# Two of the gMLP's four ways down computed with Strassen's seven products

## The chip, the cores and the metric

One Trainium2 chip, of which the kernel uses a single core. A core has five engines that each work through an instruction list of their own, in order: TensorE (matmuls, with its weight loads beside them), VectorE, ScalarE, GpSimd and SyncE, which here issues the loads from memory. They meet through semaphores. In the profile they are PE, PEld, DVE, ACT, POOL and SP. The metric is the device time of one execution in microseconds, lower is better.

## What is computed

A trunk of two layers over 512 tokens of width 1024, in fp32. Layer 0 mixes with an mLSTM, layer 1 with a chunked gMLP, and each layer has a SwiGLU FFN before and after its mixer, a gated input embedding, and a LayerNorm after every residual. The change lies in the gMLP:

```python
def gmlp_mixer(x, w_in, b_in, vn_g, vn_b, ws, bs, w_out):      # x: 1 x 512 x 1024
    u, v = jnp.split(jax.nn.gelu(x @ w_in + b_in, approximate=False), 2, axis=-1)   # 2048 each
    v = layer_norm(v, vn_g, vn_b).reshape(B, NB, GM_BLOCK, GM_GROUPS, GM_GDIM)
    s = jnp.einsum('gts,bnsgc->bntgc', ws_m, v) + bs.T[:, :, None]   # within blocks of 128 tokens
    return (u * s.reshape(B, S, GM_WIDTH)) @ w_out               # 2048 -> 1024: the way down
...
x = layer_norm(DN_ALPHA * x + mix, ln_g[i, 1], ln_b[i, 1])
```

## The kernel before

**Precision.** Every fp32 matrix is held as a high and a low half in fp32r. `split` makes them: ScalarE copies the high half, VectorE subtracts it from the source. A product of two blocks is three matmuls (`mm3`): high by high, high by low, low by high. A matmul takes a 128 x 128 block as stationary operand and 512 columns as moving one.

**Weights.** The class `Weights` streams all weights through one list, `W.order`. A load of 1 MB goes from SyncE into one of three raw buffers (`wraw`), and is cut into tiles of 1024 columns. `fill` splits the next tile of the list as soon as a split buffer is free: four of kind main and two of kind extra in this stage. `release` gives a buffer back and fills at once; with `later=True` it is only noted, and `refill` fills later. With `low="dma"` the low half is not made by VectorE: ScalarE writes the source negated and rounded, and a DMA that GpSimd issues adds the source to it. A raw buffer is free for the next load when the last tile in it is split.

**The gMLP.** First `v` for all tokens, tokens on the partitions, four column chunks by four token blocks, into `gvf`. Then 16 gate blocks of 128 channels. For block b, `spatial(b)` multiplies the split `v` by the spatial weights into two banks (`sps`), VectorE adds bias and gain in four evictions (`gs`) after one small instruction (`gadd`), and `split_v(b + 2)` splits `v` for two blocks on. `gate_u(b + 1)` then makes the next block's gate columns: 24 matmuls into one bank (`gups`), a Gelu by ScalarE (`guf`). Last `gated(b)` multiplies the two and splits the result into `hh` and `hl`. After every fourth block `down` multiplies the four blocks by their four row blocks of `w_out`: for each of four token blocks, four row blocks by two halves of 512 columns by three matmuls into two banks (`dps`), and two residual additions by VectorE into `xt`. The last way down carries the LayerNorm along.

**Banks.** PSUM has eight banks of 512 columns. Four are handed out by `up_bank` (`ps_up`, one pool of four), four by `dn_bank` (`ps_dn`), which can pin them. `spatial` takes up banks, for blocks 1, 3 and 15 down banks.

**Strassen in the other stages.** The FFNs, and the mLSTM for its first three heads, take their ways down group by group through the class `Group`. The two factors are cut two by two; seven products of half-size sums replace eight. `form` makes the next activation sum (none, one or two additions by VectorE, in place) and splits it; `W.forms` makes the seven weight sums, two of them pairs of subtractions in place in the raw buffers; `product` runs one product into two pinned banks, and `add` adds them to `xt`. One product follows each up-projection, so that these steps are spread.

Of the kernel before, what the change touches and what calls it, by code (L numbers as in the profile page):

```python
# [237 lines left out]
def hybrid_trunk(ctx: ExitStack, tc, x, p, ln_g, ln_b, ffn1_wgu, ffn1_wd, ffn2_wgu, ffn2_wd,  # L238
# [20 lines left out]
    ps_up = ctx.enter_context(tc.tile_pool(name="ps_up", bufs=4, space=PSUM))  # L259
# [15 lines left out]

    def up_bank(name):
        return ps_up.tile([P, 512], F32, name=name, tag="up")
# [31 lines left out]
    def kp(w):  # L309
        return w.rearrange("(kb p) c -> p kb c", p=P)  # L310
# [58 lines left out]

    def stage_kinds(first):  # L370

        n = len(W.order) - first
        for i in range(n):
            extra = i % 6 >= 4 if i < n // 6 * 6 else i >= n - 2
            W.order[first + i] = ("extra" if extra else "main",) + W.order[first + i][1:]

    def ml_weights():
        win, wout = ml_w_in[0], ml_w_out[0]
        first = len(W.order)
        for h in range(HEADS):  # L380
# [7 lines left out]
            if h:  # L388
# [3 lines left out]
                j0, j1 = W.add_load(kp(wout)[:, k:k + 2, :], 3), W.add_load(kp(wout)[:, k + 2:k + 4, :], 3, "gb")  # L392
                left, right = ((slice(None), slice(None), slice(c, c + 512)) for c in (0, 512))
                down_w = W.forms("", (j0, left), (j0, right), (j1, right), (j1, left))
# [9 lines left out]
    def gm_weights():  # L404
        win, wout = gm_w_in[0], gm_w_out[0]
        first = len(W.order)
        for c in range(4):
            add_wide(win, GW + c * 512)
        for b in range(16):
# [4 lines left out]
            if b and b % 4 == 0:  # L414
                add_rows(wout, b - 4, 4)
# [314 lines left out]
    class Group:  # L730
# [5 lines left out]
        def __init__(self, h, pool, first=False):  # L736
            self.h, self.pool, self.half = h, pool, h.shape[1] // 2
# [26 lines left out]
        def product(self):  # L764
# [437 lines left out]
    def gmlp():  # L1202
        with stage_pool("extra", EXTRA) as extra, stage_pool("gm_parts") as near, stage_pool("ghpool", 4) as hpool, \
                stage_pool("gm") as mp:
            W.open("extra", extra, EXTRA)
            vf = mp.tile([P, TB, GW], F32, name="gvf")
# [34 lines left out]
            for c in range(4):  # L1241
# [9 lines left out]
                for t in range(TB):  # L1251
# [4 lines left out]
                    dst = vf[:, t, c * 512:(c + 1) * 512]  # L1256
# [7 lines left out]
                    if c == 3:  # L1264
# [5 lines left out]
                        vec.tensor_scalar(vf[:, t], vf[:, t], mv[:, 0:1], rs[:, 1:2], op0=OP.subtract, op1=OP.mult)  # L1270
# [12 lines left out]
            def split_v(b):  # L1283
# [5 lines left out]
                split(vh, vl, vf[:, :, b * P:(b + 1) * P])  # L1289
# [24 lines left out]
            def gated(s, uf):  # L1314
                vec.tensor_mul(s, s, uf)
# [178 lines left out]
```

## Time and profile before

| | us |
|---|---|
| time, median of 3 runs | 2232.23 |
| lowest and highest of them | 2232.04 to 2232.97 |
| the profiled execution's own time | 2232.51 |
| its span in the profile | 2230.8 |
| TensorE busy (PE) | 2220.3 |
| VectorE busy (DVE) | 1526.0 |
| ScalarE busy (ACT) | 913.9 |

The profile is of one execution. Times in it count from the start of its span. An engine's busy time is the union of its instructions' times; matmuls overlap in the pipeline, so their recorded lengths (389 ns) are longer than the distance from one start to the next. Views show the instructions in order of time, the waits with what ended them, busy times by stretch, and the DMAs with the time to their landing.

### The profile page before, as it was taken

What the parts mean: (1) busy time and instruction counts of PE and PEld (TensorE: products, weight loads), DVE (VectorE), ACT (ScalarE), POOL (GpSimd) and SP (SyncE); (2) the same over time, 40 slices, a digit from 0 to 9 for tenths busy, and PEclk for the clock granted to TensorE, in tenths of its full rate; (3) what the DMA queues carried; (4) which work ended last, traced back from release to release, by engine and by line L of the source; (5) the groups of instructions that cost most, each with busy time, mean ns of one, the idle gap of its engine ahead of it and who ended that gap; (6) DMA issues with size and microseconds to landing.
All of it is one profiled execution on the core that took longest, in us unless ns stands there. A gap on an engine that the chain in (4) does not pass through costs nothing.

```text
span 2230.8 us, 26548 instructions
## 1 busy us (share of the span) xinstructions
PE 2220.3 (100%) x10589; PEld 1864.0 (84%) x10589; DVE 1526.0 (68%) x2240; ACT 913.9 (41%) x1298; POOL 101.8 (5%) x135
## 2 busy tenths in 40 slices
PE   9999999999999999999999999999999999999998
PEld 8888888888888888888889888888888888888887
DVE  5666667777776786666687666666666578666677
ACT  4333336454646533333255333334343453333332
POOL 1000000111101100000000000000010100000000
PEclk9999999999999999999999999999999999999999
DMA  7422323466847443332233422223355443332221
GB/s 231 130 93 88 95 85 100 100 149 135 166 107 161 123 139 126 95 104 67 95 123 122 133 86 87 93 87 109 106 142 142 104 151 123 122 113 85 85 85 57
DMA packets 202723, 253.56 MB, mean 114 GB/s; under 512 B 5812, under 2 KB 156468, under 8 KB 202600
## 3 DMA queue, kind: packets, MB, share of 16 engines
q1 hardware_dynamic: 168080, 211.83, 29.5%
q0 software_dynamic: 27904, 25.35, 7.9%
q10 hardware_dynamic: 6616, 14.69, 2.0%
q8 instruction: 83, 1.36, 0.2%
q14 instruction: 40, 0.33, 0.0%
HBM read 224.58 MB, written 2.11 MB: 102 GB/s over the span
## 4 chain that ended last, share of the span: by engine, by line
PE 99%; ACT 1%; DVE 0%; issue 0%; DVEq 0%; POOL 0%; POOLq 0%
PE fps L269 13%; PE fps L270 13%; PE fps L268 13%; PE gps L270 7%; PE gps L269 7%; PE gps L268 7%; PE dps L269 3%; PE dps L268 3%; PE dps L270 3%; PE gups L268 1%; PE vps L268 1%; PE zps L268 1%; PE zps L270 1%; PE vps L270 1%; PE gvps L268 1%; PE gups L269 1%
## 5 line engine op out<-in xcount | busy, mean ns | idle before, releaser
L268 PE MATMUL fps<-xh,whi 128*128 128x512 f32 x1312 | 510.7, 389 | 0.0
L269 PE MATMUL fps<-xl,whi 128*128 128x512 f32 x1312 | 510.5, 389 | 0.0
L270 PE MATMUL fps<-xh,wlo 128*128 128x512 f32 x1312 | 510.4, 389 | 0.0
L199 DVE TENSOR_TENSOR wlo<-wraw,whi 128x1024 fp32r<-128x1024 f32 (+1 forms) x286 | 345.4, 1218 | 149.5 <-ACT whi L193 147.8
L193 ACT ACTIVATE whi<-wraw 128x1024 fp32r<-128x1024 f32 (+1 forms) x334 | 346.5, 1048 | 185.8 <-PE fps L269 81.6
L199 DVE TENSOR_TENSOR wlo<-wquarter,whi 128x1024 fp32r<-128x1024 f32 (+1 forms) x140 | 156.5, 1118 | 218.2 <-ACT whi L193 218.2
L268 PEld LDWEIGHTS fps<-xh,whi 128*128 128x128 f32 x1312 | 246.3, 188 | 51.2
L269 PEld LDWEIGHTS fps<-xl,whi 128*128 128x128 f32 x1312 | 246.3, 188 | 51.1
L270 PEld LDWEIGHTS fps<-xh,wlo 128*128 128x128 f32 x1312 | 246.2, 188 | 51.0
L193 ACT ACTIVATE whi<-wquarter 128x1024 fp32r<-128x1024 f32 (+1 forms) x140 | 136.3, 974 | 279.8 <-PE gps L270 209.0
L270 PE MATMUL gps<-whi,flo 128*128 128x512 f32 x588 | 229.3, 390 | 0.0
L268 PE MATMUL gps<-whi,fhi 128*128 128x512 f32 x588 | 229.3, 390 | 0.0
L269 PE MATMUL gps<-wlo,fhi 128*128 128x512 f32 x588 | 229.2, 390 | 0.0
L593 DVE TENSOR_TENSOR xt<-xt,gps 128x512 f32<-128x512 f32 x282 | 180.3, 680 | 0.5 <-PE gps L270 0.5
L817 ACT ACTIVATE sg<-fps 128x512 f32<-128x512 f32 x80 | 47.9, 598 | 228.4 <-PE fps L270 228.4
L273 ACT ACTIVATE fhi<-h 128x512 fp32r<-128x512 f32 (+1 forms) x140 | 80.5, 581 | 142.9 <-DVE h L755 54.4
L269 PEld LDWEIGHTS gps<-wlo,fhi 128*128 128x128 f32 x588 | 110.4, 188 | 23.5
L268 PEld LDWEIGHTS gps<-whi,fhi 128*128 128x128 f32 x588 | 110.4, 188 | 23.3
L270 PEld LDWEIGHTS gps<-whi,flo 128*128 128x128 f32 x588 | 110.4, 188 | 23.3
L274 DVE TENSOR_TENSOR flo<-h,fhi 128x512 fp32r<-128x512 f32 (+1 forms) x140 | 87.2, 634 | 42.9 <-ACT fhi L273 42.9
L563 POOL TENSOR_TENSOR rs<-rs,eps_pow 128x1 f32<-128x1 f32 x32 | 20.6, 643 | 1556.4 <-DVE rs L562 1556.4
L466 ACT ACTIVATE xf<-xps,cols 128x128 f32<-128x128 f32 x160 | 59.8, 453 | 52.5 <-PE xps L461 52.5
(289 smaller groups left out, 3736.4 us busy)
## 6 DMA issues: line engine op xcount, KB each, us to landing
wraw<-in_ffn_wgu_dram SPq DMA_DIRECT2D x79, 1024.0 KB, 6.0
wquarter<-in_ffn_wd_dram SPq DMA_DIRECT2D x64, 512.0 KB, 3.7
wraw<-in_ml_w_in_dram SPq DMA_DIRECT2D x24, 1024.0 KB, 5.5
wlo<-wraw POOLq DMA_DIRECT2D x48, 512.0 KB, 6.5
wraw<-in_gm_w_in_dram SPq DMA_DIRECT2D x15, 1024.0 KB, 5.7
wraw<-in_ffn_wgu_dram SPq DMA_DIRECT2D x17, 512.0 KB, 4.0
wraw<-in_ffn_wd_dram SPq DMA_DIRECT2D x8, 1024.0 KB, 4.9
wraw<-in_ml_w_out_dram SPq DMA_DIRECT2D x8, 1024.0 KB, 4.9
```

The costliest lines, as they stand in the source:

```text
L193: self.nc.scalar.activation(hi[:, s], src[:, s], AF.Copy)
L199: self.nc.vector.tensor_sub(lo[:, s], src[:, s], hi[:, s].bitcast(F32))
L268: mm(ps, st[0], mv[0], start=start, stop=False, skip_group_check=more)
L269: mm(ps, st[0], mv[1], start=False, stop=False, skip_group_check=more)
L270: mm(ps, st[1], mv[0], start=False, stop=stop, skip_group_check=more)
L273: sca.activation(hi, src, AF.Copy)
L274: vec.tensor_sub(lo, src, hi.bitcast(F32))
L466: sca.activation(xf[:, k], ps[:, k], AF.Identity, scale=col("ln_g", norm.at + 4 * g + k), bias=col("ln_b", norm.at + 4 * g + k))
L563: pool.tensor_tensor(rs[:, 1:2], rs[:, 0:1], eps_pow, op=OP.pow)
L593: vec.tensor_add(dst, dst, ps)
L817: sca.activation(sg, ps, AF.Silu)
```

## The change

- The first eight gate blocks, two groups of four, go down by `Group`'s seven products each. `GM_STEPS` says how many products follow the gate columns of each block: one after blocks 3, 4, 6 and 8 to 12, two after blocks 5, 7 and 13. The activations are cut by tokens (`by_tokens`), the row blocks of `w_out` into left and right halves of two loads, both into raw buffers.
- `gated` writes its product in place of `v` in `gvf`, which is cut into three tiles, so that blocks 10 to 13 can reuse the first two for `h`. From block 8 on `split_gated` splits; `h` has two pairs of buffers of its own where it had four, and blocks 14 and 15 use the forms' buffers.
- In blocks 1 to 12 the weight buffers are noted as free (`later=True`) and filled a block later, after the next block's spatial part.
- The third way down (blocks 8 to 11) comes after block 13, where it came after block 11.
- `up_bank` names its four banks and hands them out in turn; `stage_kinds` marks main and extra by another formula.

```diff
-    ps_up = ctx.enter_context(tc.tile_pool(name="ps_up", bufs=4, space=PSUM))
+    ps_up = ctx.enter_context(tc.tile_pool(name="ps_up", bufs=1, space=PSUM))
...
+    up_order = deque(range(4))
+
     def up_bank(name):
-        return ps_up.tile([P, 512], F32, name=name, tag="up")
+        up_order.rotate(-1)
+        return ps_up.tile([P, 512], F32, name=name, tag=f"up{up_order[-1]}")
...
+    GM_STEPS = {3: 1, 4: 1, 5: 2, 6: 1, 7: 2, 8: 1, 9: 1, 10: 1, 11: 1, 12: 1, 13: 2}
+    GM_LAST = max(GM_STEPS)
...
-            extra = i % 6 >= 4 if i < n // 6 * 6 else i >= n - 2
+            extra = i % 6 >= 4 if i < n - 4 else i >= n - 2
...
+    def two_row_forms(w, kind="raw"):
+        j0, j1 = W.add_load(w[:, :2], 3), W.add_load(w[:, 2:], 3, kind)
+        left, right = ((slice(None), slice(None), slice(c, c + 512)) for c in (0, 512))
+        return W.forms("", (j0, left), (j0, right), (j1, right), (j1, left))
...
-            if b and b % 4 == 0:
-                add_rows(wout, b - 4, 4)
+        tiles = W.order[at:]
+        del W.order[at:]
+        down_w, k = deque(), 0
+        for b, tile_b in enumerate(tiles):
+            W.order.append(tile_b)
+            for _ in range(GM_STEPS.get(b - 1, 0)):
+                if not down_w:
+                    down_w.extend(two_row_forms(kp(wout)[:, k:k + 4, :]))
+                    k += 4
+                W.order.append(down_w.popleft())
+            if b == GM_LAST + 1:
+                add_rows(wout, 8, 4)
...
+                if self.by_tokens:
+                    return self.h[:, 2 * i - 2:2 * i, (j - 1) * 256:j * 256]
...
-                    mm3(ps, [a[:, k, e * P:(e + 1) * P] for a in f], [a[:, k] for a in w],
+                    i, j = (e, k) if self.by_tokens else (k, e)
+                    mm3(ps, [a[:, i, j * P:(j + 1) * P] for a in f], [a[:, k] for a in w],
...
-            vf = mp.tile([P, TB, GW], F32, name="gvf")
+            vfs = [mp.tile([P, TB, n], F32, name="gvf", tag=f"gv{i}") for i, n in enumerate((512, 512, 1024))]
...
-                        vec.tensor_scalar(vf[:, t], vf[:, t], mv[:, 0:1], rs[:, 1:2], op0=OP.subtract, op1=OP.mult)
+                        for v in vfs:
+                            vec.tensor_scalar(v[:, t], v[:, t], mv[:, 0:1], rs[:, 1:2], op0=OP.subtract, op1=OP.mult)
...
-            def gated(s, uf):
-                vec.tensor_mul(s, s, uf)
-                h = new_h(hpool)
-                split(h[0], h[1], s)
-                return h
+            def gated(b, s, uf):
+                s, uf = (a.rearrange("p (t c) -> p t c", t=TB) for a in (s, uf))
+                vec.tensor_mul(v_block(b), s, uf)
+
+            def split_gated(b):
+                if b < 10:
+                    h = new_h(hpool)
+                elif b < 14:
+                    if b % 2 == 0:
+                        h2.append(mp.tile([P, 4, SEQ], F32R, name="h2", tag=f"gv{b // 2 - 5}"))
+                    k = b % 2 * 2
+                    h = [h2[-1][:, i] for i in (k, k + 1)]
+                else:
+                    h = [fpool.tile([P, 2, 256], F32R, name=n, tag=n).rearrange("p t c -> p (t c)") for n in ("fhi", "flo")]
+                split(*(a.rearrange("p (t c) -> p t c", t=TB) for a in h), v_block(b))
+                hs.append(h)
...
             for b in range(16):
+                add()
                 if b in (0, 14):
                     ss.extend(spatial(i, vs.popleft()) for i in (b, b + 1))
-                    if b == 0:
-                        W.refill(2)
-                        W.release(2, low="dma")
                 elif b not in (1, 15):
                     ss.append(spatial(b, vs.popleft()))
-                ahead = 0 < b < 15
-                if ahead:
+                if b == 0:
+                    W.refill(2)
+                    W.release(2, later=True)
+                else:
+                    W.refill(1 if b == 1 else len(W.held), "dma")
+                if 0 < b < 15:
                     us.append(gate_u(b + 1))
-                hs.append(gated(ss.popleft(), us.popleft()))
-                if ahead and b < 14:
-                    W.release(low="dma")
+                gated(b, ss.popleft(), us.popleft())
+                if b in (2, 3):
+                    form()
+                n = GM_STEPS.get(b, 0)
+                for i in range(n):
+                    if i:
+                        add()
+                    products.popleft().product()
+                    form()
+                if b >= 8:
+                    split_gated(b)
+                if b == GM_LAST:
+                    W.release()
+                    W.release(n, low="dma")
+                    add()
+                    down(hs[:4], False)
+                elif 0 < b < GM_LAST:
+                    W.release(1 + n, later=True)
                 elif b == 15:
                     W.release()
-                if b % 4 == 3:
-                    down(hs, b == 3, Norm(1, 1) if b == 15 else None)
-                    hs = []
+                    down(hs[4:], False, Norm(1, 1))
```

## Rows read from the trace of the kernel before

**Rows 1.** The page: the chain that ended last, by engine.
```profile
PE 99%; ACT 1%; DVE 0%; issue 0%; DVEq 0%; POOL 0%; POOLq 0%
```

**Rows 2.** Windows, a way down, four blocks: PE, PEld, DVE, ACT, POOL; PEclk; DMA; GB/s.
```profile
1652.40:1674.20 21.80, 21.80 (x98) 18.06 (x97) 7.84 (x11) 6.29 (x7) 1.60 (x2) 1.00 0.77 168
1674.20:1699.70 25.50, 25.50 (x130) 21.66 (x129) 18.87 (x35) 12.56 (x17) 3.28 (x3) 1.00 0.59 159
```

**Rows 3.** TensorE in order of time: start, length, line, names, shapes.
```profile
1632.30 0.28 PE L1300 MATMUL sps<-wsp,gvh 128*128 128x256 f32 x1
...
1639.60 0.28 PE L1300 MATMUL sps<-wsp,gvh 128*128 128x256 f32 x1
...
1652.37 0.39 PE L268 MATMUL dps<-whi,hh 128*128 128x512 f32 x1
...
1674.13 0.28 PE L1300 MATMUL sps<-wsp,gvh 128*128 128x256 f32 x1
...
1680.52 0.28 PE L1300 MATMUL sps<-wsp,gv 128*128 128x256 f32 x1
...
1686.90 0.28 PE L1300 MATMUL sps<-wsp,gvh 128*128 128x256 f32 x1
```

**Rows 4.** VectorE in order of time in the gate blocks; idle time in brackets.
```profile
1630.99 0.69 DVE L274 TENSOR_TENSOR gvl<-gvf,gvh 128x512 fp32r<-128x512 f32 x1 [0.70 <-ACT gvh L273]
...
1638.22 2.35 DVE L199 TENSOR_TENSOR wlo<-wraw,whi 128x1024 fp32r<-128x1024 f32 x2
...
1644.47 0.35 DVE L1303 SCALAR_TENSOR_TENSOR gadd<-rsum,cols 128x128 f32<-128x128 f32 x1
...
1646.75 0.68 DVE L274 TENSOR_TENSOR gvl<-gvf,gvh 128x512 fp32r<-128x512 f32 x1
1647.35 0.69 DVE L1315 TENSOR_TENSOR gs<-gs,guf 128x512 f32<-128x512 f32 x1
1648.73 0.69 DVE L274 TENSOR_TENSOR hl<-gs,hh 128x512 fp32r<-128x512 f32 x1 [0.70 <-ACT hh L273]
...
1676.62 1.28 DVE L591 SCALAR_TENSOR_TENSOR xt<-xt,dps 128x512 f32<-128x512 f32 x2
1677.82 0.34 DVE L1303 SCALAR_TENSOR_TENSOR gadd<-rsum,cols 128x128 f32<-128x128 f32 x1
```

**Rows 5.** VectorE in order of time in the mLSTM: weight form, then activation form.
```profile
562.67 1.22 DVE L105 TENSOR_TENSOR wraw<-wraw 128x1024 f32<-128x1024 f32 x1
...
566.27 1.22 DVE L199 TENSOR_TENSOR wlo<-wraw,whi 128x1024 fp32r<-128x1024 f32 x1 [1.12 <-ACT whi L193]
567.45 0.06 DVE L959 MEMSET pad<- 128x3 f32 x1
...
575.78 0.68 DVE L754 TENSOR_TENSOR hf<-hf 128x512 f32<-128x512 f32 x1
576.50 0.69 DVE L755 TENSOR_TENSOR hf<-hf 128x512 f32<-128x512 f32 x1
...
578.50 1.28 DVE L593 TENSOR_TENSOR xt<-xt,gps 128x512 f32<-128x512 f32 x2
```

**Rows 6.** ScalarE in order of time: the two passes over a gate tile.
```profile
1643.73 1.05 ACT L193 ACTIVATE whi<-wraw 128x1024 fp32r<-128x1024 f32 x1
1644.69 1.04 ACT L196 ACTIVATE wlo<-wraw 128x1024 fp32r<-128x1024 f32 x1
```

**Rows 7.** DMAs of the stage: a SyncE issue; medians; landings of subtractions, then loads.
```profile
1639.46 6.46 SPq L162 DMA_DIRECT2D wraw<-in_gm_w_in_dram  x2
...
wraw<-in_gm_w_in_dram SPq DMA_DIRECT2D x13, 1024.0 KB, 5.9
wraw<-in_gm_w_out_dram SPq DMA_DIRECT2D x8, 1024.0 KB, 4.9
...
DMA to landing us min/median/max: 4.5/6.4/10.2
...
DMA to landing us min/median/max: 3.7/5.3/9.9
```

More of the change, by code (lines that the diff above doesn't have):

```diff
@@ L391, in ml_weights @@
                 k = 4 * h - 4
-                j0, j1 = W.add_load(kp(wout)[:, k:k + 2, :], 3), W.add_load(kp(wout)[:, k + 2:k + 4, :], 3, "gb")
-                left, right = ((slice(None), slice(None), slice(c, c + 512)) for c in (0, 512))
-                down_w = W.forms("", (j0, left), (j0, right), (j1, right), (j1, left))
+                down_w = two_row_forms(kp(wout)[:, k:k + 4, :], "gb")
                 for i, tile_i in enumerate(tiles):
@@ L408, in gm_weights @@
             add_wide(win, GW + c * 512)
+        at = len(W.order)
         for b in range(16):
@@ L734, in hybrid_trunk, with __init__ @@
         TO = ((0, 0), (0, 0), (0, 1), (1, 1), (1, 1), (0, 1), (1, 0))
-        def __init__(self, h, pool, first=False):
-            self.h, self.pool, self.half = h, pool, h.shape[1] // 2
+        def __init__(self, h, pool, first=False, by_tokens=False):
+            self.h, self.pool, self.half, self.by_tokens = h, pool, h.shape[1] // 2, by_tokens
             self.first = (0, 2, 3, 6) if first else ()
@@ L1202, in gmlp, with v_cols, v_block @@
     def gmlp():
-        with stage_pool("extra", EXTRA) as extra, stage_pool("gm_parts") as near, stage_pool("ghpool", 4) as hpool, \
-                stage_pool("gm") as mp:
+        with stage_pool("extra", EXTRA) as extra, stage_pool("gm_parts") as near, stage_pool("ghpool", 2) as hpool, \
+                stage_pool("forms", 2) as fpool, stage_pool("gm") as mp:
             W.open("extra", extra, EXTRA)
-            vf = mp.tile([P, TB, GW], F32, name="gvf")
+            vfs = [mp.tile([P, TB, n], F32, name="gvf", tag=f"gv{i}") for i, n in enumerate((512, 512, 1024))]
+            def v_cols(c, n):
+                i = min(c // 512, 2)
+                return vfs[i][:, :, c - 512 * i:c - 512 * i + n]
+            def v_block(b):
+                return v_cols(b * P, P)
             wsp = near.tile([P, GRP, 2, P], F32R, name="wsp")
@@ L1255, in gmlp @@
                     up_tokens(t, ws, ps, hook=run_hook if t else None, release=give_back)
-                    dst = vf[:, t, c * 512:(c + 1) * 512]
+                    dst = v_cols(c * 512, 512)[:, t]
                     vec.tensor_add(dst, ps, vb)
@@ L1288, in split_v @@
                     vl = near.tile([P, TB, P], F32R, name="gvl", tag="gvl")
-                split(vh, vl, vf[:, :, b * P:(b + 1) * P])
+                split(vh, vl, v_block(b))
                 return vh, vl
@@ L1312, in spatial, with form, add @@
                 return s
-            def gated(s, uf):
-                vec.tensor_mul(s, s, uf)
-                h = new_h(hpool)
-                split(h[0], h[1], s)
-                return h
+            def gated(b, s, uf):
[13 more added lines that the diff above has]
+                hs.append(h)
+            groups = [Group(vfs[g], fpool, g == 0, True) for g in range(2)]
+            h2 = []
+            forms, products, added = (deque(g for g in groups for _ in range(7)) for _ in range(3))
+            def form():
+                if forms:
+                    forms.popleft().form()
+            def add():
+                if len(added) > len(products):
+                    added.popleft().add()
             vs = deque([split_v(0), split_v(1)])
```

## The prediction

> **What bounds the kernel now.** I read the chain that ended last first: 99% of the span is TensorE, spread over the matmul lines of every stage [rows 1]. Then the busy time of the engines by stretch, to see whether the stage that the change touches is any different: in a way down and in the four gate blocks behind it TensorE is busy for the whole of each stretch (21.80 of 21.80 us, 25.50 of 25.50), at the full granted clock, while VectorE has 7.84 and 18.87 us of work [rows 2]. So time is what TensorE is given to do, and a change in this stage gains what it takes off TensorE, less what TensorE comes to wait for. VectorE is what could make it wait: about a quarter of it is idle in the blocks and two thirds in a way down, and the change moves the ways down into the blocks.
>
> The prices are steps from start to start. A way down is 96 matmuls from 1652.37 to 1674.13, so one takes 0.2267 us; a gate block is 6.38 us from one `sps` to the next, of which 24 matmuls make 5.44 and the spatial part the other 0.94 [rows 3]. On VectorE [rows 4] a block costs 2.28 for `gadd` and the four evictions and 0.60 for the low half of `v` (2.9 in all), 0.60 for the product with `guf`, 0.60 for a low half of `h` with 0.70 of idling ahead of it while ScalarE copies the high half, 1.2 for a pair of residuals, and 1.13 for the low half of a weight tile (two in 2.35, less one's 1.22).
>
> **The change part by part.** *TensorE.* A product is 2 banks by 2 blocks by 3 matmuls of the same shape as now, 12 in all. Seven make 84 where the group now has 96. Two groups save 24 matmuls: 24 x 0.2267 = 5.44 us. A block with n products is 6.4 + 2.7n us long: 6.4 for block 2, 11.8 for blocks 5, 7 and 13, 9.1 for the other eight.
>
> *VectorE.* The trace has the same helpers in the mLSTM [rows 5]. A weight form that is made (two sums, ScalarE's copy, the low half) holds VectorE from 562.67 to 567.45, 4.8 us; four of the fourteen are such, the others cost 1.1. An activation form costs 2.7 where it needs two sums, 2.0 where one, 0.6 where none. In the stage this is 12 more residuals (7.2), six more splits of `h` or a form (3.6), six more weight tiles (6.8), eight sums of weights (10) and eight of `h` (5.6): some 33 us more, though two of the ways down that were its rest are gone.
>
> Block by block VectorE then has, from block 2 to block 12, with its pieces in the order of the code (residuals, evictions, weight tiles, product, forms, split): 5.2, 11.6, 10.1, 11.0, 7.6, 8.2, 13.9, 10.7, 8.4, 8.4 and 7.0 us. Block 8, the dearest, is 1.2 + 2.9 + 1.1 + 4.8 + 0.6 + 2.7 + 0.6. TensorE has 6.4, 9.1, 9.1, 11.8, 9.1, 11.8, then five times 9.1. The sums are 102 and 103 us, so VectorE has no slack to speak of, and its lateness is what counts.
>
> *Waits that come with it.* ScalarE works its list in order, and so does VectorE. At block 2 form 1 needs the second half of the four row blocks. Its load can go out only when the low half of gate column 4 is done, 1639.46 now [rows 7]; at 4.9 us for a load of `gm_w_out` [rows 7] and 1.05 for the copy [rows 6], VectorE idles some 0.9. Behind that copy stand ScalarE's two passes over gate column 6 (0.96 each [rows 6]) and a Gelu, and then the first form's high half, for which VectorE idles 1.3 more. The same order costs 1.3 at block 4, and a fresh source 0.7 at block 3. At block 10 column 13 must be copied before form 4; its load waits for the subtraction by DMA of column 12, copied in block 9 (6.4, then 5.9 for the load [rows 7]); worked through that queue, VectorE idles 2.2.
>
> How late may VectorE be? It frees both spatial banks 3.6 us into its block (1.2 + 2.3 + 0.1), and TensorE asks for the second of them 0.9 into its next block, since a block takes three of the four banks. So it may start a block P - 2.7 late, P being the block's length: 6.4 with one product, 9.1 with two. What exceeds that TensorE waits. It now starts block 2 at 1644.47 against `sps` at 1639.60, 4.9 late [rows 3, 4]; two splits of `h` and their idling go away (2.6), which leaves 2.3. From there, lateness plus work plus idling less P: 3.3 at block 3, 6.5 at block 4 (0.1 over), 8.7 at 5, 7.9 at 6 (1.5 over), 4.9 at 7, 1.3 at 8, 6.1 at 9, 7.7 at 10 (1.3 over), 7.9 at 11 (1.5 over), 5.7 at 12, 3.6 at 13. TensorE waits 0.1 + 1.5 + 1.3 + 1.5 = 4.4 us.
>
> *The end.* The third way down now stands right before blocks 14 and 15. After a way down VectorE is 3.7 us late (`sps` at 1674.13, `gadd` at 1677.82 [rows 3, 4]), since the freed weight buffers and two residuals come first. Then come two blocks' evictions (4.6), two products, two splits with their idling: the low half of block 15 is ready 12.3 us after `sps`. TensorE gets there after two spatial parts, 5.5 of gate columns and 20 matmuls, 11.7 us: a wait of 0.6. Now a whole gate block lies between.
>
> *Edits that I cost at nothing.* The banks in turn: TensorE waits for no bank in the stretches read [rows 2], so there is nothing to gain; if another stage met a bank out of turn it would wait for an eviction (0.68 us), and I see no reason for one. `gvf` in three tiles makes three instructions of one, four times; the first low half ends at 1631.68 and is asked for from 1632.30 [rows 3, 4], so 0.6 us covers it, and ScalarE's copy need wait only for the first third, which may gain as much. The main and extra marks come out the same for both lists. The loads are as many megabytes as before, eight of `gm_w_out`.
>
> *A rule against a row.* Subtractions by DMA landed in 4.5 to 10.2 us, median 6.4, and loads in 3.7 to 9.9 [rows 7]. The Trainium skill, "DMA: Bandwidth & Descriptors", section "Issuing engines are not separate DMA queues", says that transfers started by different engines run on the same 16 DMA engines and interleave. By that rule a subtraction and a load in flight together share, and the sum would lie nearer the long ends than the medians that I use: 2238 in place of 2231.8 (the third case below). The spread of the landings agrees with it.
>
> **The sum.** -5.44 + 4.4 + 0.6 = -0.4 us. The profiled execution took 2232.51, which would become 2232.1; it lies 0.28 over the median of the runs shown, so the median of 2232.23 becomes 2231.8.
>
> **The rivals.** *The cover holds.* If copies and loads come in time, so that the 0.9, 1.3, 0.7, 1.3 and 2.2 of idling vanish, lateness runs 2.3, 1.1, 3.6, 4.6, 3.8, 2.3, 0, 4.8, 6.4, 5.7 and never passes its limit. Only the end's 0.6 stays: 2227.4. For it speaks that my limits are missed by 1.5 at most; against it that idling ahead of low halves stands in every block of the trace [rows 4, 5]. It decides below 1.0 us of waits in all. Without even the end's wait it is 2226.8, the floor.
>
> *The gate columns' only buffer.* The two halves of the row blocks hold two of three raw buffers for most of seven products, so gate columns pass through one. From copying column 12 to having column 13: two passes of ScalarE, 6.4, a load of 5.9, two passes, 6.4, some 22.5 us. TensorE asks for it three blocks and 0.9 later (28.2), plus its own waits there (2.8), less ScalarE's lateness (6.1): 24.9, a slack of 2.4. With landings at the long ends (10.2, 9.9, 10.2) the chain is 11.6 longer and TensorE waits 9 us at one place; taking two thirds of that, the time is 2238. This is the slower side, and it decides once the three landings together pass some 21 us by 4.5. For it speaks that each transfer waits for the one ahead, so they seldom overlap less than now; against it that the rows tiles no longer go by DMA in this stretch, so there are fewer.
>
> *It does not save the matmuls' time.* If products ran slower than ways down, nothing would be saved and the waits remain: 2237. The mLSTM's and the FFN's products have the same shape and run on the same saturated TensorE [rows 1], so this is unlikely.
>
> **How the numbers follow.** The forecast has 0.60, the cover that holds 0.20, the one buffer 0.16, no saving 0.04. A change of under 0.2% (4.5 us) can hardly be told from none here. Faster is the second case, 0.20; slower the last two, 0.20; within 0.2% the forecast, 0.60, whose own range (waits of 2 to 9 us) is 2229 to 2236. The range reaches from the cover that holds to the one buffer at two thirds: 2227.4 to 2238.
>
> **What would show it.** Right: `gps` matmuls of 12 to a product at 0.227 between the gate blocks; waits of TensorE of 0.5 to 1.5 us at the second spatial bank or the gate columns of blocks 5 to 13, with VectorE's evictions as their releaser; VectorE near 95% busy or idling only for ScalarE between blocks 3 and 12; a short wait at the last way down. Wrong: no wait of TensorE in the stage (second case); a wait of several us on a `wlo` that a DMA finishes (third case); a longer span in a stage that is not the gMLP, which would point to the banks.

## The result, and the profile after

The changed kernel takes 2239.96 us (median of 8 runs, 2236.96 to 2240.51) against 2232.26 (8 runs, 2232.03 to 2233.32) of the kernel before. The ratio of the means is 1.0029, 95% interval 1.0019 to 1.0040; the ratios further down are of means too. It is slower by 0.3%, which lies outside the range of the prediction. Its runs form two groups, three at 2237.0 to 2237.3 and five at 2239.7 to 2240.5; the profiled one took 2237.32 us with a span of 2235.6, 4.8 more than before.

First the page of the changed kernel: busy time, then the chain that ended last, as in [rows 1].

```profile
PE 2218.6 (99%) x10565; PEld 1859.6 (83%) x10565; DVE 1557.9 (70%) x2288; ACT 923.2 (41%) x1310; POOL 104.5 (5%) x135
...
PE 88%; DVE 5%; DMA 3%; ACT 2%; issue 2%; POOL 0%; SPq 0%; DVEq 0%; ACTq 0%; POOLq 0%
```

The chain is no longer TensorE alone: in the gMLP it runs through VectorE, ScalarE and DMAs. The waits of TensorE in that stage (who waits, for whom, us in total, times, longest) and TensorE and VectorE in order of time say where:

```profile
PE sps L1339 <- DVE gs L1348: 4.8, 4, 2.0
PE gups L268 <- DVE gs L1348: 1.1, 4, 0.3
```

```profile
1639.33 0.28 PE L1339 MATMUL sps<-wsp,gvh 128*128 128x256 f32 x1
...
1718.13 0.22 PE L1340 MATMUL sps<-wsp,gvl 128*128 128x128 f32 x1
1720.04 0.36 PE L1339 MATMUL sps<-wsp,gvh 128*128 128x256 f32 x1 [1.69 <-DVE gs L1348]
...
1721.28 0.63 PE L269 MATMUL gups<-xl,whi 128*128 128x512 f32 x1
1721.70 0.63 PE L270 MATMUL gups<-xh,wlo 128*128 128x512 f32 x1
...
1742.57 0.35 PE L1339 MATMUL sps<-wsp,gvh 128*128 128x256 f32 x1 [1.96 <-DVE gs L1348]
...
1751.75 0.28 PE L1339 MATMUL sps<-wsp,gv 128*128 128x256 f32 x1
```

```profile
1641.67 0.34 DVE L1342 SCALAR_TENSOR_TENSOR gadd<-rsum,cols 128x128 f32<-128x128 f32 x1
...
1702.06 0.35 DVE L1342 SCALAR_TENSOR_TENSOR gadd<-rsum,cols 128x128 f32<-128x128 f32 x1
...
1712.10 1.22 DVE L199 TENSOR_TENSOR wlo<-wraw,whi 128x1024 fp32r<-128x1024 f32 x1 [3.54 <-ACT whi L193]
...
1718.44 0.34 DVE L1342 SCALAR_TENSOR_TENSOR gadd<-rsum,cols 128x128 f32<-128x128 f32 x1
...
1735.35 1.23 DVE L199 TENSOR_TENSOR wlo<-wraw,whi 128x1024 fp32r<-128x1024 f32 x1 [3.13 <-ACT whi L193]
...
1756.07 1.28 DVE L617 TENSOR_TENSOR xt<-xt,gps 128x512 f32<-128x512 f32 x2
```

Four rows give the whole balance. `sps` starts block 2 at 1639.33 and block 13 at 1751.75: TensorE needs 112.4 us for blocks whose matmuls make 102.8 by the prediction's prices (6.4 + 8 x 9.1 + 2 x 11.8, which it rounds to 103), so 9.6 are lost. VectorE starts block 2 with `gadd` at 1641.67 and block 13 with the residuals at 1756.07: it takes 114.4 us for the same eleven blocks, where the prediction had 102.1 of work and 6.4 of idling. (VectorE is busy for 91.8 of the 114.4; the prediction's 102.1 holds the short waits for ScalarE that come with the splits.) The waits stand at the second spatial bank of blocks 5, 7, 10 and 12 and at the gate columns behind it. Counted as delay against the usual step they are 1.2, 1.0, 2.2 and 2.5 us, 6.8 in all; the brackets of the rows hold the idle time alone. Behind the one at block 10 the matmuls step by 0.427 us in place of 0.227, for eight of them, which is 1.6 us. The 1.2 us left are small delays here and there. In the windows of that stretch and of the one behind the wait at block 12 (busy time of PE, PEld, DVE, ACT, POOL; granted clock; DMA; GB/s) the clock is 0.50, which is the 1.2 GHz level, and 1.00:

```profile
1721.20:1724.60 3.40, 3.40 (x9) 2.65 (x9) 2.56 (x3) 0.77 (x1) 0.00 (x0) 0.50 1.18 134
1743.40:1747.00 3.60, 3.52 (x16) 2.94 (x17) 2.87 (x4) 0.61 (x2) 0.00 (x0) 1.00 1.15 148
```

The step of 0.427 us is the figure that the Trainium skill, "TensorE: Matmul & The Clock Gate", section "Wait — 56ns, not 53.3ns?", gives for 512 columns at the lower level (426.7 ns); the trace agrees.

The span adds up. The 24 matmuls that are gone make -5.4, blocks 2 to 12 +9.6, and the last way down +0.9: its first twelve matmuls on blocks 14 and 15, which are split only just before, take 3.67 us (1795.36 to 1799.03) in place of 2.72. Block 2 starts 0.3 us earlier than before (1639.33 against 1639.60 [rows 3]). Together that is +4.8, and 4.8 was measured.

VectorE's longest block is the eighth, 16.4 us from 1702.06 to 1718.44. It stands 3.54 us for ScalarE's copy of weight form 2. ScalarE, GpSimd and SyncE show what is behind that:

```profile
1709.12 1.06 ACT L193 ACTIVATE whi<-wraw 128x1024 fp32r<-128x1024 f32 x1 [6.95 <-DMA wraw<-in_gm_w_in_dram]
1710.08 1.04 ACT L196 ACTIVATE wlo<-wraw 128x1024 fp32r<-128x1024 f32 x1
1711.03 1.04 ACT L193 ACTIVATE whi<-wraw 128x1024 fp32r<-128x1024 f32 x1
```

```profile
1694.76 1.53 POOL L197 DMA_DIRECT2D wlo<-wraw  x1 [3.22 <-DVE gs L1346]
```

```profile
1703.39 0.37 SPq L162 DMA_DIRECT2D wraw<-in_gm_w_in_dram  x1
```

Read backward: the form's copy (1711.03) stands behind gate column 11 in ScalarE's list (1709.12), which waits for its load; the load went out at 1703.39, when the adding DMA of column 10, issued at 1694.76, had left the raw buffer, 8.6 us later. At block 10 the same chain, with columns 12 and 13, makes the 3.13.

### The profile page after: what moved, and what is told of

It reads as the page before. It is cut to its first block, busy times and chain, and to the rows that moved or that the text cites. A ratio compares the mean times of both kernels' runs of the same rounds, so it can differ in the third digit from the quotient of the medians.

```text
span 2235.6 us, 26582 instructions
## 1 busy us (share of the span) xinstructions
PE 2218.6 (99%) x10565; PEld 1859.6 (83%) x10565; DVE 1557.9 (70%) x2288; ACT 923.2 (41%) x1310; POOL 104.5 (5%) x135
## 4 chain that ended last, share of the span: by engine, by line
PE 88%; DVE 5%; DMA 3%; ACT 2%; issue 2%; POOL 0%; SPq 0%; DVEq 0%; ACTq 0%; POOLq 0%
PE fps L268 13%; PE fps L270 13%; PE fps L269 13%; PE gps L270 7%; PE gps L268 7%; PE gps L269 7%; PE dps L270 2%; PE dps L268 2%; PE dps L269 2%; PE vps L268 1%; PE zps L268 1%; PE zps L270 1%; PE vps L270 1%; PE zps L269 1%; PE vps L269 1%
## 5 line engine op out<-in xcount | busy, mean ns | idle before, releaser
L199 DVE TENSOR_TENSOR wlo<-wraw,whi 128x1024 fp32r<-128x1024 f32 (+1 forms) x292 | 352.6, 1218 | 157.3 <-ACT whi L193 156.3
L193 ACT ACTIVATE whi<-wraw 128x1024 fp32r<-128x1024 f32 (+1 forms) x340 | 352.1, 1048 | 189.3 <-PE fps L269 81.6
L268 PE MATMUL gps<-whi,fhi 128*128 128x512 f32 x644 | 251.1, 390 | 0.0
L270 PE MATMUL gps<-whi,flo 128*128 128x512 f32 x644 | 251.1, 390 | 0.0
L269 PE MATMUL gps<-wlo,fhi 128*128 128x512 f32 x644 | 251.0, 390 | 0.0
L617 DVE TENSOR_TENSOR xt<-xt,gps 128x512 f32<-128x512 f32 x302 | 193.0, 680 | 0.5 <-PE gps L270 0.5
L269 PEld LDWEIGHTS gps<-wlo,fhi 128*128 128x128 f32 x644 | 120.9, 188 | 25.7
L268 PEld LDWEIGHTS gps<-whi,fhi 128*128 128x128 f32 x644 | 120.9, 188 | 25.6 <-issue 0.3
L270 PEld LDWEIGHTS gps<-whi,flo 128*128 128x128 f32 x644 | 120.9, 188 | 25.6
L587 POOL TENSOR_TENSOR rs<-rs,eps_pow 128x1 f32<-128x1 f32 x32 | 20.6, 644 | 1574.3 <-DVE rs L586 1574.3
```

The source lines that it names most:

```text
L193: self.nc.scalar.activation(hi[:, s], src[:, s], AF.Copy)
L199: self.nc.vector.tensor_sub(lo[:, s], src[:, s], hi[:, s].bitcast(F32))
L268: mm(ps, st[0], mv[0], start=start, stop=False, skip_group_check=more)
L269: mm(ps, st[0], mv[1], start=False, stop=False, skip_group_check=more)
L270: mm(ps, st[1], mv[0], start=False, stop=stop, skip_group_check=more)
L587: pool.tensor_tensor(rs[:, 1:2], rs[:, 0:1], eps_pow, op=OP.pow)
```

## The experiments

Two theories stood at first. *Load:* VectorE loses its lead where it stands behind ScalarE, which stands for loads that an adding DMA holds up. *Work:* VectorE has more to do in these blocks than there is time, wherever it stands. A third: the fall of the clock is what costs.

**1. Two gate columns by VectorE.**

```diff
             W.order.append(tile_b)
+            if b in (10, 12):
+                W.in_place.add(tile_b[2])
```

> The changed kernel, but VectorE makes the low halves of gate columns 10 and 12 itself (two subtractions of 1.2 us) in place of a negated copy by ScalarE and an adding DMA. Load theory (VectorE loses its lead because it stands, 3.54 us in block 8 and 3.13 in block 10, behind ScalarE, which waits for the load of the next pair of gate columns, and that load for the adding DMA that has the buffer): the two loads go out some 6 to 8 us earlier, both idle times go, TensorE's waits at the spatial products of blocks 10 and 12 (1.81 + 0.38 and 2.07 + 0.38 us) and the low clock behind the first (1.6) go with them: about 2231 us. Work theory (VectorE's added work alone uses up the lead): 2.1 to 2.4 us more of its work, so the waits stay or grow: 2237 to 2242.

Measured 2235.08 us (11 runs, 2233.43 to 2235.49), ratio 1.0011 [1.0002, 1.0020]. The load of columns 11 and 12 went out at 1699.48, 3.9 us earlier (6 to 8 were expected), the long idle times were gone (in block 8 1.13 us is left, for ScalarE's copy alone), and the wait at block 12 too; that at block 10 fell to 0.28 + 0.38. But a new one of 2.33 + 0.38 stood at block 11, for which the 2.4 us of work taken over suffice. Neither theory held alone. The three lowest runs, the profiled one among them, are at 2233.5, 3.7 under the lower group of the changed kernel, where the load theory had 6.2. With 6.7 us of standing gone and 2.4 of work added one would have 4.3, so the time fits standing and work that count alike; it does not prove it.

**2. Without the sums of weight quarters.**

```diff
         def t2():
-            vec.tensor_sub(raw(b12), raw(b22), raw(b12))
-            vec.tensor_add(raw(b11), raw(b12), raw(b11))
             return raw(b11), ()
         def t1():
-            vec.tensor_sub(raw(b21), raw(b21), raw(b11))
-            vec.tensor_sub(raw(b11), raw(b22), raw(b11))
             return raw(b11), (b11[0],)
```

The diff is shown as it acts on the gMLP's two groups; the other stages keep their sums.

> The changed kernel without the eight sums of weight quarters (1.22 us each on VectorE) of the gMLP's two groups: the products use the loaded quarters as they are, so the output is not the reference's. Work theory: 4.9 us less VectorE work for each group, all four waits of TensorE at the spatial products (blocks 5, 7, 10, 12; 6.4 us) and the low clock (1.6) go: about 2229 us. Load theory: only the waits of blocks 5 and 7 (1.19 + 0.98 us), which have no load behind them, go; in blocks 8 and 10 VectorE stands longer behind ScalarE instead, and the waits at blocks 10 and 12 and the clock stay: about 2235 us.

2229.14 us (11 runs, 2228.91 to 2229.77), ratio 0.9986 [0.9977, 0.9995]: the number of the work theory. VectorE stood even longer at one place (6.14 us, behind the load of column 13), yet only one wait was left, 1.15 + 0.38 us at block 12, which the work theory did not have. With enough lead the standing is covered. This run changes VectorE's time and no bank, and it follows the prediction's limit: VectorE starts block 11 at 1731.86 against `sps` at 1723.95, 7.9 us late where 6.4 are allowed, and the 1.5 us over are the wait at block 12; no block before it is over. TensorE, then VectorE:

```profile
1723.95 0.28 PE L1341 MATMUL sps<-wsp,gv 128*128 128x256 f32 x1
...
1734.66 0.35 PE L1341 MATMUL sps<-wsp,gvh 128*128 128x256 f32 x1 [1.04 <-DVE gs L1350]
```

```profile
1731.86 1.28 DVE L619 TENSOR_TENSOR xt<-xt,gps 128x512 f32<-128x512 f32 x2
```

**3. Spare matmuls in the waits.**

```diff
+                if b in (10, 12):
+                    for _ in range(15):
+                        mm(banks[0][:, 0], vh[:, 0], wsp[:, g], start=True, stop=False, skip_group_check=True)
```

> The changed kernel, with 15 spare matmuls of 256 columns (some 1.7 us) ahead of the spatial products of blocks 10 and 12, into the bank that those products then start afresh, so that TensorE works in most of the time that it waited in. Clock theory (a wait of about 2 us is followed by a stretch at 1.2 GHz, worth 1.6 us each time it comes): the waits become work, nothing is lost to it, and no stretch at half clock follows: 2235.5 us in all runs, and the 3 us between the two clusters of times of the changed kernel are gone. Rival (the wait and its price are one, the clock is no term, or the fall comes from elsewhere): the times stay at 2237 and 2240, or grow by what the spare matmuls add.

2237.51 us (11 runs, 2236.87 to 2238.59), ratio 1.0023 [1.0015, 1.0032]. One group of times instead of two, and no stretch at half clock: so far as expected. But not 2235.5: a wait of 1.15 + 0.38 us appeared at block 11, where the profile without fillers has none. Full clock gained nothing there, since TensorE only came sooner to a bank that VectorE had not read.

**4. The small edits on the kernel before.**

```diff
+    up_order = deque(range(4))
     def up_bank(name):
-        return ps_up.tile([P, 512], F32, name=name, tag="up")
+        up_order.rotate(-1)
+        return ps_up.tile([P, 512], F32, name=name, tag=f"up{up_order[-1]}")
...
-            vf = mp.tile([P, TB, GW], F32, name="gvf")
+            vfs = [mp.tile([P, TB, n], F32, name="gvf", tag=f"gv{i}") for i, n in enumerate((512, 512, 1024))]
```

> The kernel before, with three of the change's edits alone: the four upward banks named in turn, the gate values in three tiles instead of one (three normalising operations in place of one for each block of tokens), and no Strassen group. If these edits cost what they were priced at, nothing: 2232.2 us, within 0.2. Rival (a bank taken in turn waits for a reader that a free choice of bank went round): a wait for each turn that meets a busy bank, some us over the whole kernel, 2234 or more.

2232.47 us (11 runs), ratio 1.0001 [0.9992, 1.0010]: nothing, as priced.

**5 and 6. The sums on GpSimd.**

```diff
-        vec = self.nc.vector
+        vec = eng or self.nc.vector      # eng = GpSimd for the gMLP's two groups
```

> The changed kernel, with the eight sums of weight quarters of the gMLP's two groups on GpSimd in place of VectorE (1.22 us each there); all else the same. Their operands are ready a block earlier, so GpSimd, which has little else to do, can make them ahead. Work theory (VectorE's lead is used up by these 9.8 us together with the standing behind loads): the time of the run that left the sums out, 2229.1 us, and one wait of about 1.5 us left at block 12, behind the load. Rival 1 (GpSimd takes several times VectorE's 1.22 us, or slows VectorE while it works): ScalarE's pass over the sum comes late, VectorE stands behind it, and the waits come back: 2236 us or more. Rival 2 (the sums were only the half that counts, the load the other): 2233 to 2235.

> The sums of weight quarters on GpSimd, and the low halves of gate columns 10 and 12 on VectorE (as in the first experiment), both at once. With the sums away VectorE has 9.8 us to give and takes back 2.4; the loads of the next columns go out 6 us earlier. Theory (work and load add): no wait of TensorE above 0.4 us is left, no stretch at the lower clock: 2227 to 2228 us. Rival (the price of the sums was all of it): no gain over the run with the sums on GpSimd alone, or 1 to 2 us more.

2243.40 us (5 runs), ratio 1.0049 [1.0036, 1.0061], and with the columns 2242.86 (5 runs), 1.0043 [1.0030, 1.0055]. GpSimd, then VectorE, of the first of the two:

```profile
1649.12 3.04 POOL L105 TENSOR_TENSOR wraw<-wraw 128x1024 f32<-128x1024 f32 x1
1652.23 2.73 POOL L106 TENSOR_TENSOR wraw<-wraw 128x1024 f32<-128x1024 f32 x1
```

```profile
1649.03 3.69 DVE L274 TENSOR_TENSOR flo<-gvf,fhi 128x512 fp32r<-128x512 f32 x1 [1.16 <-ACT fhi L273]
1652.64 2.48 DVE L1342 SCALAR_TENSOR_TENSOR gadd<-rsum,cols 128x128 f32<-128x128 f32 x1
1655.22 0.48 DVE L1346 SCALAR_TENSOR_TENSOR gs<-sps,cols,gadd 128x256 f32<-128x256 f32 x1
```

A sum takes GpSimd 2.4 to 3.0 us against 1.22, and VectorE's operations on two tiles of SBUF stretch while it lasts: 3.69 for 0.69, 2.48 for 0.35; the eviction from PSUM behind them took its 0.48. The Trainium skill, "SBUF — State Buffer", section "SBUF: two separate sides", says that the two engines share a port pair as an exclusive lock, which a VectorE operation with two SBUF inputs needs too; these rows agree. Nor could GpSimd work ahead: in block 8 its sums began at 1710.38, behind an adding DMA that waited in its list for the late column, and VectorE idled 8.38 us. Here work that left VectorE for GpSimd took VectorE's time all the same.

**7. Deliberate waits in the kernel before.**

```diff
+            def stall(ps, n):
+                d = mp.tile([P, P], F32R, name="stall", tag="gadd", bufs=2)
+                mm(ps[:, :P], wsh[:, 0], wsh[:, 0], start=True, stop=True)
+                sca.activation(d, ps[:, :P], AF.Copy)
+                for _ in range(n):
+                    sca.activation(d, d, AF.Copy)
+                mm(ps[:, :P], d, wsh[:, 0], start=True, stop=True)
```

> The kernel before, with three deliberate waits of TensorE, ahead of the gate columns 5, 8 and 11: a matmul of 128 columns into the bank of that column, two, five and nine copies by ScalarE of 128x128 one after the other, and a matmul that reads the last; the column then starts the bank afresh. By ScalarE's rows of smaller shapes a chain of these is some 0.8, 1.6 and 2.7 us. Clock theory: behind the waits of 1.6 us and more, or some of them, TensorE goes at 1.2 GHz for eight or so matmuls (1.6 us lost), in some executions and not in others, so the times fall into clusters 1.6 us apart; behind the shortest never: 2237.4 us without a fall, 2239 with one, 2240.6 with two. Rival (a wait costs itself and no more): one cluster at 2237.4.

2249.11 us (5 runs, 2247.80 to 2250.24), ratio 1.0075 [1.0061, 1.0088]. The chains queued behind ScalarE's other work, so TensorE waited 1.4, 4.4 and 5.8 us, more than was planned, and the 2237 is void. Windows behind the second, third and first wait:

```profile
1700.40:1703.60 3.20, 3.20 (x10) 2.48 (x10) 0.00 (x0) 0.00 (x0) 0.00 (x0) 0.53 1.27 257
1748.90:1751.50 2.60, 2.60 (x7) 2.12 (x8) 0.00 (x0) 0.00 (x0) 0.00 (x0) 0.50 0.46 66
1676.00:1680.00 4.00, 3.74 (x17) 3.11 (x18) 3.81 (x9) 0.20 (x1) 0.00 (x0) 1.00 1.02 334
```

Behind the two long waits the clock is at half, behind the short one at full. With no change of the gMLP at all, a wait alone brought the fall. The five times spread over 2.4 us without clear groups, so the clusters of the expectation stay open.

**8. The changed kernel again, for a second profile.**

> The changed kernel as it is, for a second profile of it. Clock theory: if this execution is of the cluster at 2240.3 us, it shows a stretch at half clock behind both of the waits of about 2 us (blocks 10 and 12), 3.2 us in all; if of the one at 2237.2, one stretch. Rival: the same stretches in both, and the 3 us lie elsewhere, in a longer wait or a later load.

2239.15 us (one run), between the two groups. Here the clock held behind the wait of block 10 and fell behind that of block 12:

```profile
1720.80:1724.60 3.80, 3.57 (x16) 3.01 (x17) 3.04 (x4) 0.69 (x1) 0.14 (x1) 1.00 1.02 116
1743.70:1747.00 3.30, 3.26 (x8) 2.64 (x9) 2.83 (x4) 0.36 (x1) 0.00 (x0) 0.50 1.14 149
```

```profile
PE sps L1339 <- DVE gs L1348: 6.0, 5, 2.2
PE gups L268 <- DVE gs L1348: 1.3, 5, 0.3
```

One stretch in either profile, and yet 1.8 us between them. The fifth wait is the answer: 1.19 + 0.38 us at block 11, just what the 1.6 us of half clock at that place had taken in the first profile: from `sps` of block 2 to that of block 12 the two take 100.7 and 100.6 us. A fall where VectorE was late anyway cost nothing; a fall behind the last wait, at block 12, cost its 1.5 us in full. This is also what the fillers showed.

**9 and 10. The forms' low halves by adding DMAs.**

```diff
-        for _, make in made:
-            self.in_place.add(make)
+        for i, (_, make) in enumerate(made):
+            if i not in by_dma:                  # (1, 4, 5, 6) for the gMLP's groups
+                self.in_place.add(make)
```

> The changed kernel, but of the quarters that a group of the gMLP uses as they are, the low halves of forms 1, 4, 5 and 6 are made as those of the gate columns are (a negated copy by ScalarE, 1.04 us, and an adding DMA) wherever the refill allows it: seven subtractions of 1.22 us less on VectorE, seven adding DMAs more. Work theory: VectorE is the bound from block 2 to block 12, so 8.5 us less work takes up to 8.5 us of waits away: 2230 to 2232 us, nearly the run without sums (2229.1). Rival 1 (the standing behind loads alone counts, and more adding DMAs make the landings longer, so the loads later): 2238 us or more. Rival 2 (the products' low halves land late, 8 to 10 us after the issue): waits of TensorE on the low half, from the DMA, in place of those on VectorE: 2236 to 2240.

> As the run before it, and gate columns 10 and 12 by VectorE besides: VectorE has 6.1 us less work than in the changed kernel, and the loads of columns 11 and 13 no longer wait for an adding DMA of the buffer that they go into. Theory (work and standing add up on VectorE, which sets the pace): 8.5 - 2.4 us of work and 6.7 us of standing go, so no wait of TensorE is left but the last way down's 0.9: 2227.5 to 2229 us, faster than both kernels. Rival (the load is free of the matter once the work is less): 1 to 2 us slower than the run without these two columns. Rival 2 (landings of the new adding DMAs): waits on low halves, 2232 or more.

2249.35 us (5 runs), ratio 1.0072 [1.0060, 1.0085], and 2237.30 with the columns (11 runs), 1.0022 [1.0013, 1.0031]. Neither came near 2230. The waits of the ninth:

```profile
PE sps L1340 <- DVE gs L1349: 6.9, 3, 5.2
PE gps L270 <- DMA wlo<-wraw: 2.1, 2, 1.4
PE dps L269 <- DVE xt L618: 1.6, 1, 1.6
PE dps L270 <- DMA wlo<-wraw: 1.1, 1, 1.1
```

Between 1686 and 1700 four adding DMAs and two loads went out, landing after 8.0 to 10.9 us, ScalarE stood 6.8 us for the next gate columns, and VectorE behind it 9.1. The mechanisms of both rivals were at work: less work on VectorE was worth nothing where it lengthened the chain of the raw buffer. The columns alone took 12 us of that back; the longest wait left in the tenth, 2.5 us, is for a low half by DMA, as its rival 2 had it.

**11 to 13. One bank for a block's spatial product.** This takes VectorE's work without touching a DMA, a buffer of weights or a queue. It has a second effect: a block then asks for two of the four banks in place of three, so VectorE may also be later than before. The same edit on the kernel before is the control.

```diff
-                    mm(ps, vh[:, t], wsp[:, g], start=True, stop=False)
-                    mm(ps[:, 1], vl[:, t], wsh[:, g], start=False, stop=True)
+                    mm(ps[:, t], vh[:, t], wsh[:, g], start=True, stop=False)
+                    mm(ps[:, t], vh[:, t], wsl[:, g], start=False, stop=False)
+                    mm(ps[:, t], vl[:, t], wsh[:, g], start=False, stop=True)
...
-                for e, ps in enumerate(banks):       # two evictions for each of two banks
...
+                vec.scalar_tensor_tensor(s.rearrange("p (t c) -> p t c", t=TB), ps, col("vn_g", b),
+                                         add[:, None, :].to_broadcast([P, TB, P]), op0=OP.mult, op1=OP.add)
```

> The changed kernel, but a block's spatial product adds its three matmuls for each 128 tokens up in one 128x128 piece of one bank (three matmuls of 128 columns in place of one of 256 and one of 128), so that VectorE reads one 128x512 bank with one operation (by the row of its 128x512 operations 0.69 us) in place of four of 0.48 (1.83 us from first to last): 1.15 us less for each block, 12.6 us over blocks 2 to 12, with no DMA, buffer or queue touched. Work theory: more than the waits' 6.8 us is taken off the engine that sets the pace, so no wait is left but the load's at block 12 (1.5 as in the run without sums): 2226.8 + 0.9 + 1.5 = 2229.2 us, plus what the third matmul costs TensorE, 0 to 0.6 us a block, which the control tells. Load theory (only the standing counts): the waits at blocks 10 and 12 stay above 1 us each, 2234 us or more.

> The one bank for a block's spatial product, and gate columns 10 and 12 subtracted by VectorE, which lets the loads of columns 11 and 13 go 6 to 8 us earlier. Theory: VectorE has 10.2 us less to do than in the changed kernel and stands nowhere for a load after block 2; no wait of TensorE is left but 0.9 us in the last way down: 2227.7 us plus the third matmul's cost; faster than the kernel before if that is under 4.5 us. Rival: the run with one bank alone is as fast, the load being covered once VectorE has its lead.

> Control: the kernel before, with the same one bank for a block's spatial product. There TensorE waited for VectorE in the gMLP nowhere by more than 0.3 us, so VectorE's 1.15 us a block are worth nothing and the difference is the third matmul's cost on TensorE alone: 0 to 0.6 us a block, 2232.3 to 2242 us. Rival (VectorE's work was already part of the pace before): faster than 2232.

Measured: 2234.03 us (11 runs), ratio 1.0008 [1.0000, 1.0017]; with the columns 2234.20 (11 runs), 1.0010 [1.0001, 1.0019]; control 2239.34 (6 runs), 1.0031 [1.0019, 1.0043]. The eviction, in VectorE's order of time, and the window of the stretch that the waits stood in, of the first of the three:

```profile
1703.28 0.75 DVE L1344 SCALAR_TENSOR_TENSOR gs<-sps,cols,gadd 128x512 f32<-128x512 f32 x1
1703.95 0.68 DVE L274 TENSOR_TENSOR gvl<-gvf,gvh 128x512 fp32r<-128x512 f32 x1
```

```profile
1653.00:1740.00 87.00, 87.00 (x439) 73.81 (x438) 63.79 (x91) 44.60 (x58) 12.31 (x8) 1.00 0.65 127
```

VectorE has 63.79 us of work in 87, TensorE is busy in all of it, and no wait is left, though VectorE still stands 4.43 us for ScalarE at one place. The third matmul costs 2239.34 - 2232.3 = 7.0 us on TensorE: three steps of 0.11 us for each 128 tokens, where the pair of 256 and 128 columns took 0.23 (0.17 and 0.06). Against its own control the change is worth 2234.03 - 2239.34 = -5.3 us: the 5.44 of the prediction, all but 0.1. The load's rival in the twelfth is right: once VectorE has its lead, earlier loads add nothing.

**14 and 15. Relief at chosen places.** Fourteen has the columns of the first experiment and the one bank in five blocks; fifteen has it in two, and makes the sums of `gadd` ahead of the blocks.

```diff
+    ONE_BANK = (3, 4, 8, 9, 10)          # fifteen: (3, 9)
...
-                add = mp.tile([P, P], F32, name="gadd", tag="gadd", bufs=2)
-                vec.scalar_tensor_tensor(add, rsum[:, g], col("vn_b", b), bsb[:, g], op0=OP.mult, op1=OP.add)
+                add = (rsum, bsb)[b % 2][:, g]           # fifteen only
```

> The changed kernel with gate columns 10 and 12 by VectorE, and the one bank for the spatial product in blocks 3, 4, 8, 9 and 10 alone. The control priced the third matmul at 7.0 us for 16 blocks, 0.44 us a block; VectorE has 1.15 us a block less. In the run with the columns alone TensorE waited 0.56 + 0.38, 0.59 + 0.38, 0.28 + 0.38 and 2.33 + 0.38 us at blocks 5, 7, 10 and 11, 5.3 us in all. If VectorE's time and nothing else makes them, 2.3 us less by block 5 clear the first two (1.9) and 3.45 us less by block 11 the others (3.4): 2232.3 - 5.4 + 5 x 0.44 = 2229.1 us, up to 0.9 more for the last way down, faster than the kernel before by 2 to 3 us. Rival (a wait comes back in another block, where the lead is used up an instruction earlier): 2231 to 2233.

> The changed kernel with gate columns 10 and 12 by VectorE, the one bank in blocks 3 and 9 alone, and the sixteen small sums of row sums and biases (0.45 us each from start to next start) made ahead, in the third column group of the gate values, in place of one in each block. By block 5 VectorE has 1.15 + 0.9 us less, by block 11 another 1.15 + 2.7: 1.9 and 3.4 us of waits are to be cleared. TensorE's price is 2 x 0.44. If all waits go: 2232.3 - 5.4 + 0.9 = 2227.8 us. Rivals: the sums made ahead keep VectorE late in the gate values' stage, where it has some 3.5 us of work for 5.4 of TensorE's, and TensorE waits there: 1 to 3 us more; or a wait stays at block 5 or 11: up to 1 us more.

Fourteen: 2229.77 us (11 runs, 2229.50 to 2230.03), ratio 0.9988 [0.9980, 0.9997]. Its chain is TensorE's again, and its window has no wait, with VectorE still at 74.48 us of 87:

```profile
PE 99%; ACT 1%; DVE 0%; issue 0%; DVEq 0%; POOL 0%; POOLq 0%
```

```profile
1653.00:1740.00 87.00, 87.00 (x428) 73.48 (x427) 74.48 (x112) 45.57 (x61) 9.31 (x6) 1.00 0.61 124
```

It beats both kernels, by 2.5 us (0.11%) and by 10, and lies where it was expected (2229.1, up to 0.9 more). The bank that the edit sets free was not needed for that: VectorE starts no block with one product more than 6.2 us late (block 10, 1722.99 against `sps` at 1716.83) and none with two more than 6.3, inside the prediction's 6.4 and 9.1 for three banks a block. Fifteen: 2232.02 us (11 runs, 2230.98 to 2234.05), ratio 0.9999 [0.9990, 1.0008]. No wait was left in blocks 2 to 13, but TensorE waited 2.0 us where the row sums now came too early for VectorE, and 1.4 at the first blocks: the first rival.

## Why the prediction was wrong, point by point

**The matmuls (-5.44).** Right: -5.3 against the control.

**The waits (+4.4).** Wrong in size, and this is the step that failed: 9.6 us. The mechanism is as foretold, down to the releaser, the second spatial bank and the gate columns. The ledger can be redone from the rows: time lost = lateness at block 2 + VectorE's time - TensorE's 102.8 - lateness at block 13. Predicted that is 2.3 + 108.5 - 102.8 - 3.6 = 4.4, measured 2.3 + 114.4 - 102.8 - 4.3 = 9.6. The equation holds whatever the cause is; that it is VectorE's time, runs two and fourteen show. So the term mis-sized is VectorE's time in blocks 2 to 12, by 5.9 us, and most of that is its idling: 11.2 us where 6.4 were counted. The largest part is block 8, 13.9 predicted and 16.4 measured: ScalarE's wait for the load of columns 11 and 12 was not in it, though the same chain was worked out for column 13 two blocks on. There too 2.2 became 3.1. Block 2 idled 1.77 and 1.16 where 0.9 and 1.3 were counted, and block 12 idled 0.70 ahead of a split where none was. The work itself was priced well: block 3 came out at 12.4 for 12.3, and over the program VectorE is busy 31.9 us more (1526.0 to 1557.9) where some 33 were added up. With 102 us of work for 103 of cover, 5.9 us more on VectorE became 5.2 more on TensorE.

**The limit to VectorE's lateness** held. At blocks 4, 6, 9 and 11 VectorE started 7.6, 7.5, 8.6 and 9.0 us late, 1.2, 1.1, 2.2 and 2.6 over the 6.4 that are allowed, and TensorE was held by 1.2, 1.0, 2.2 and 2.5 at blocks 5, 7, 10 and 12. (Block 10 is 10.3 late by its start, but TensorE lost 3.9 within it.) Block 9 was too late where block 10 was expected to be, because of block 8.

**The rivals.** The third, the gate columns' only buffer, was half right. Its chain is what made block 8 long, with two adding DMAs and a load under way together that landed after 8.5 to 10.4 us; that is the side to which the rule had pointed that the prediction takes from the Trainium skill, "DMA: Bandwidth & Descriptors", section "Issuing engines are not separate DMA queues". But TensorE never waited for that `wlo` by more than 0.2 us: from column 10 to 11 and from 12 to 13 the three landings together took 20.6 and 21.0 us, and the rival needed more than some 21. ScalarE's order passed the delay on to VectorE. The cover that holds (2227.4) is what the kernel does with a VectorE that has its lead: run fourteen without its third matmuls' price (5 x 0.44) is at 2227.6.

**The clock.** The prediction did not have it. It explains the two groups in part: shown are one fall without net cost (first profile) and one that cost 1.5 us (second). The profiled run, 2237.32, lies inside the prediction's range; it is the upper group that puts the median past 2238. No profile fell in that group, so that its runs have both falls, or one more, is argued and not shown, and the cause of its last 2.4 to 3.2 us stays open.

**The end (+0.6)** measured 0.9. **The edits at nothing:** the banks in turn and the three tiles cost 0.15 us, inside the interval; the marks were not run apart.

## What to carry to other kernels

Before moving work into a stage, add up the engine beside the bound one, its standing included: with work at 99% of the cover, nearly all that it lost was paid (5.2 of 5.9 us). Take work off that engine outright (fewer, wider operations) rather than hand it to GpSimd or a DMA, for here both took it back through a port or a buffer. And price relief with a control: a third matmul was worth its price in 5 blocks, not in 16.

## What was not expected of the hardware

Behind a wait of TensorE the granted clock fell to half in some executions and not in others. In the changed kernel it was 0.50 behind the wait of block 10 in one profile and 1.00 in the next, and the other way round at block 12, with waits of 1.8 to 2.3 us. Behind a wait of 1.5 us at block 5 it was 0.50 in the ninth run and 1.00 in the tenth. While GpSimd summed two tiles of SBUF, a 0.69 us operation of VectorE took 3.69. Adding DMAs that met loads and one another landed after 8 to 11 us where before the median was 6.4 and the longest 10.2 [rows 7].
